# Layer 0's output weights split at later places, and layer 1's scores in fewer, wider products

## The chip, the cores and the metric

The kernel runs on one core of one Trainium2 chip. The metric is the device time of one execution in microseconds (us). The kernel before takes 779.3 us, the median of three runs (778.96 to 779.54).

## The reference, cut to what matters

The model is a two-layer backbone over 512 latent tokens and 256 context tokens with 1024 features. Layer 0 mixes latent attention (8 heads, softmax over all 768 tokens) with a bidirectional recurrence, gates both, and multiplies the 1024 mixed features by an output matrix. Layer 1 is a neighbourhood attention with 16 heads of 64: each latent token attends to a window of its grid (8 rows by 16 columns) and to all 256 context tokens, in one softmax:

```python
y_l = jnp.concatenate([o_l * jax.nn.silu(g_mla[:, c_:]), r_l * jax.nn.silu(g_lru[:, c_:])], axis=-1) @ w_out   # layer 0
...
s_loc = jnp.einsum('bhqd,bhrqcd->bhqrc', q_row, k_win) + bias                                                  # layer 1
s_ctx = jnp.einsum('bhqd,bhkd->bhqk', q_row, k_c)
s = jnp.concatenate([s_loc.reshape(b_, NA_HEADS, GRID_W, n_loc), s_ctx], axis=-1)
p = jax.nn.softmax(s.astype(jnp.float32), axis=-1)
```

## The kernel before, in words

All matrix products keep nearly float32 precision by splitting every operand into a high part (rounded by ScalarE, "ACT") and a low part (the remainder, subtracted by VectorE, "DVE", or by GpSimd, "POOL"). A product is then three products of TensorE ("PE"): high by high, high by low, low by high. Weights come from HBM as raw tiles by DMAs that SyncE's queue ("SP") issues, `load_w`, and are split by `split_raw`.

Raw weight tiles live in a pool with the tag "r", which has three buffers; high and low parts have the tags "h" and "l" with four buffers each. Layer 0's attention uses the same three tags in turn for its transposed probabilities (`pt_tile`, line 837: "rhl" by a running number). A tile takes a buffer when one is free.

Layer 0's attention runs head by head. `scores(hd, qt)` makes the products into PSUM (line 808), the row maximum on DVE (line 810), the exponential on ACT (line 812), and the normalization on POOL (line 764). `tail(hd, half, i)` takes one step of `mla_tail`: four transposes on PE (line 881), the split of the transposed tile on ACT (line 843) and DVE (line 844), and the products with the values (lines 861 and 862). The last step of a head combines the halves (lines 757 to 759) into the feature tile `mix`. `split0(p)` splits feature tile p into `mh` and `ml`; tile 3 comes from heads 6 and 7 and is the last. Between these calls stand the preparations of the output weights: the matrix is cut into four quarters `w0o[0]` to `w0o[3]` of 256 output features, each loaded and split in two pieces of four feature tiles (`w0o00`, `w0o04`) or in three pieces of three (`w0o20`, `w0o23`, `w0o26`). `out0(q, c)` then multiplies (line 1175), in the order of feature tiles 4, 5, 6, 7, 0, 1, 2, 3: the first four come from the recurrence and are ready early, so that these products can run between the last steps of the attention.

Layer 1's `scores1(hd, b)` handles 128 queries. `q2` holds their high and their low part in two slots, each doubled over both halves of the 128 rows; `k2` holds 512 latent and then 256 context keys, the high part in one half of the rows and the low part in the other. So each slot of `q2` meets both parts of the keys at once: 256 latent keys (line 1346) and the 256 context keys (line 1347), in two products into one PSUM tile of 512 columns. For b under 3 the latent keys are one stretch of 256; for b = 3 they are the first and the last 128.

The calls stand in a long hand-written order. A planner with its own model of time then orders the instructions of each engine: what stands earlier in the program goes first, but an instruction that the model holds to be not ready yet lets later ones pass. After that each engine works through its list strictly in order. `behind(ACT)` adds one rule: what is traced inside it on ACT comes after the ACT instruction traced last before it. `go(key)` runs a generator to its next `yield`, so a piece of work can be started in one place and continued in others.

Of the kernel before, what the change touches and what calls it, by code (L numbers as in the profile page):

```python
# [22 lines left out]
NL = 512  # L23
# [23 lines left out]
def build(nc, tc, A, out, dbg=None):  # L47
# [4 lines left out]
    V, S, P, G, SY = nc.vector, nc.scalar, nc.tensor, nc.gpsimd, nc.sync  # L52
    PE, ACT, DVE = mybir.EngineType.PE, mybir.EngineType.Activation, mybir.EngineType.DVE

    def f(ap):
        return ap.bitcast(F32)

    def dump(name, ap):
        if dbg is not None and name in dbg:
            SY.dma_start(dbg[name], ap)  # L60
# [14 lines left out]
    def tile3(p, tag, dt=F32, bufs=None):  # L75
        return lambda name, dt=dt: p.tile([128, NT], dt, tag=tag, name=name, bufs=bufs)
# [6 lines left out]
    th = tile3(ph, "th")  # L83

    def t4(name, shape=(1024,), dt=F32, tag="r", p=None):
        t = (p or pc).tile([128, 1024], dt, tag=tag, name=name, bufs=(PA if p else PC)[tag])
        n = int(np.prod(shape))
        if len(shape) == 1:
            return t[:, :n]
        names = "abc"[: len(shape)]  # L90
        return t[:, :n].rearrange(
            f"p ({' '.join(names)}) -> p {' '.join(names)}", **dict(zip(names, shape))
        )
# [3 lines left out]
    def small(tag, name, n=1, dt=F32):  # L97
        return sm.tile([128, n], dt, tag=tag, name=name, bufs=SM.get(tag))
# [14 lines left out]
    def load_w(name, src, shape, new=None):  # L113
        raw = (new or t4)(name + "r", shape, F32, "r")
        SY.dma_start(raw, src)
        return raw

    def split_raw(name, raw, shape, new=None, eng=V, heng=S):
        hi = (new or t4)(name + "h", shape, F32R, "h")
        if heng is S:  # L120
            S.activation(hi, raw, AF.Copy)
        else:
            heng.tensor_copy(hi, raw)
        lo = (new or t4)(name + "l", shape, F32R, "l")
        eng.tensor_tensor(lo, raw, f(hi), ALU.subtract)
        return hi, lo

    def split_w(name, src, shape, new=None, eng=V, heng=S):
        return split_raw(name, load_w(name, src, shape, new), shape, new, eng, heng)
# [68 lines left out]
    def behind(*engines):  # L198

        stack = ExitStack()  # L200
        for e in engines:
            stack.enter_context(tc.issue_after(next(i for i in reversed(nc.cur_bb.bb.instructions) if i.engine == e)))
        return stack
# [64 lines left out]
    def of3(tile):  # L268
        def new(n, s, dt, tag):
            if tag == "r":  # L270
                return t4(n, s, dt, tag)
            return tile(n, dt)[:, : s[0] * s[1]].rearrange("p (a b) -> p a b", b=s[1])

        return new
# [135 lines left out]
    def go(key, new=None):  # L410

        if new is not None:
            going[key] = new
        next(going[key], None)
# [85 lines left out]
    nl, e, z, w, q = (small("sp", f"sp{i}", 8) for i in range(5))  # L500
# [260 lines left out]
    def softmax_tail(p, rsum, name):  # L761
        rc = small("rc", name, 1)
        V.reciprocal(rc, rsum)  # L763
        G.tensor_scalar(p, p, rc, 0.5, ALU.mult, ALU.mult)  # L764
# [35 lines left out]
    def scores(hd, qt):  # L800
        qh, ql = qs[hd]
        kh, kl = KH[hd % 2], KL[hd % 2]
        if qt < 4:
            s = zz(f"s{hd}{qt}")
            qc = slice(128 * qt, 128 * qt + 128)
            for i, (a, b) in enumerate(((qh, kh), (qh, kl), (ql, kh))):
                for c in (LAT, CTX):
                    P.matmul(s[:, c], a[:96, qc], b[:96, c], start=(i == 0), stop=(i == 2))  # L808
            nm, rsum = small("nm", f"nm{hd}{qt}"), small("rs", f"rs{hd}{qt}")
            V.tensor_reduce(nm, s[:, :NT], AX.X, ALU.max, negate=True)  # L810
            p = th(f"p{hd}{qt}")
            S.activation(p, s[:, :NT], AF.Exp, bias=nm, accum_out=rsum)  # L812
            softmax_tail(p, rsum, f"rc{hd}{qt}")
            pts[hd, qt] = p
            return
        s = zz(f"sc{hd}")[:, :512]
        for qt in range(2):
            qc = slice(NL + 128 * qt, NL + 128 * qt + 128)
            for i, (a, b) in enumerate(((qh, kh), (qh, kl), (ql, kh))):
                P.matmul(  # L820
                    s[:, 256 * qt : 256 * qt + 256], a[:96, qc], b[:96, CTX],
                    start=(i == 0), stop=(i == 2),
                )
        nm, rsum = small("nm", f"nmc{hd}", 2), small("rs", f"rsc{hd}", 2)
        V.tensor_reduce(nm, s.rearrange("p (a b) -> p a b", a=2), AX.X, ALU.max, negate=True)
        p = ptmp.tile([128, 512], F32, tag="pcx", name=f"pc{hd}", bufs=1)
        for qt in range(2):
            S.activation(
                p[:, 256 * qt : 256 * qt + 256], s[:, 256 * qt : 256 * qt + 256], AF.Exp,
                bias=nm[:, qt : qt + 1], accum_out=rsum[:, qt : qt + 1],  # L830
            )
            softmax_tail(p[:, 256 * qt : 256 * qt + 256], rsum[:, qt : qt + 1], f"rcc{hd}{qt}")
        pts[hd, 4] = p
# [134 lines left out]
    v_t(5)  # L968
    scores(0, 2)
    mh, ml = [None] * 8, [None] * 8  # L970
    def wo_prep(l, name, q, new=None, step=4, eng=V, heng=S):
        w = []
        for k in range(0, 8, step):
            n = min(step, 8 - k)
            h, lo = split_w(f"{name}{q}{k}", A["wo"][l, q, :, k : k + n], (n, 256), new, eng, heng)
            w += [(h[:, i], lo[:, i]) for i in range(n)]
        return w

    def split0(p):
        mh[p], ml[p] = tl(f"mh{p}", F32R), (tl if p == 4 else tmix)(f"ml{p}", F32R)  # L980
        S.activation(mh[p], mix[p], AF.Copy)
        (V if p == 3 else G).tensor_tensor(ml[p], mix[p], f(mh[p]), ALU.subtract)
# [3 lines left out]
    def tail(hd, half, i):  # L986
        if i == 0:
            tails[hd, half] = mla_tail(hd, half)
        next(tails[hd, half], None)
# [7 lines left out]
    w0o = {}  # L997
# [6 lines left out]
    def w0o_prep(q, new=None, step=4):  # L1004
        w0o[q] = wo_prep(0, "w0o", q, new, step, G if q == 0 else V)
# [98 lines left out]
    tail(5, 1, 0)  # L1104
    tail(5, 1, 1)
    scores(6, 4)
    w0o_prep(0)
    split0(1)
    tail(5, 1, 2)
    go("a3")  # L1110
# [8 lines left out]
    scores(7, 2)  # L1119
    split0(7)  # L1120
    tail(6, 0, 2)
    tail(6, 0, 3)
    tail(6, 1, 0)
    tail(6, 1, 1)
    tail(6, 1, 2)
    tail(6, 1, 3)
    split0(2)
    scores(7, 3)
    scores(7, 4)
    w0o_prep(2, of3(th), 3)  # L1130
    tail(7, 0, 0)
    tail(7, 0, 1)
    tail(7, 0, 2)
    tail(7, 0, 3)
    tail(7, 1, 0)
    tail(7, 1, 1)
    tail(7, 1, 2)
    tail(7, 1, 3)
    split0(3)
    for p in range(8):  # L1140
        dump(f"mix{p}", mix[p])

# [11 lines left out]
    def st(name):  # L1154
        return ps_.tile([128, 512], F32, tag="s", name=name)
# [71 lines left out]
        w = (LAT, CTX)[c]  # L1227
        h_block(1, j, c, x1[j][:, w], rsb1[:, w], hh1[j], hl1[j], PIECES[c])

    w0o_prep(1)  # L1230
    out0(0, 0)
    w0o_prep(3, of3(tl), 3)
    out0(2, 0)
# [16 lines left out]
    def t2(tag, name, dt=F32, bufs=None):  # L1250
        return pn2.tile([128, 512], dt, tag=tag, name=name, bufs=bufs)
# [79 lines left out]

    p1 = {}

    def scores1(hd, b):
        q2, k2 = qk[hd], ke1[hd // 2][hd % 2]
        bt = bias[hd % 2]
        if b == 0:
            SY.dma_start(bt[:, :2], A["bias"][hd])
        s = st(f"s1{hd}{b}")
        for i in range(2):  # L1340
            lhs = q2[:, i, 128 * b : 128 * b + 128]
            if b < 3:
                kap = k2[:, 128 * b : 128 * b + 256]
            else:
                kap = k2[:, :NL].rearrange("p (a b) -> p a b", b=128)[:, ::3]
            P.matmul(s[:, :256], lhs, kap, start=(i == 0), stop=False, skip_group_check=True)  # L1346
            P.matmul(s[:, 256:], lhs, k2[:, CTX], start=False, stop=(i == 1), skip_group_check=True)  # L1347
        nm, rsum = small("nm", f"nm1{hd}{b}"), small("rs", f"rs1{hd}{b}")
        bb = bt[:, 0::2] if b < 3 else bt[:, 1:3]
        sv = s.rearrange("p (a b) -> p a b", b=256)  # L1350

        V.tensor_tensor_reduce(sv, sv, bb, -1.0, 3e38, ALU.add, ALU.min, nm)  # L1352
        p = t2("p", f"p1{hd}{b}", bufs=6)
        S.activation(p, s, AF.Exp, bias=nm, scale=-1.0, accum_out=rsum)  # L1354
        softmax_tail(p, rsum, f"rc1{hd}{b}")
        p1[hd, b] = p
# [45 lines left out]
    def w1o_prep(q, new=None, step=4, **kw):  # L1402
        w1o[q] = wo_prep(1, "w1o", q, new, step, **kw)
# [47 lines left out]
    v_t1(0, 4)  # L1451
    k1(0)
    scores1(0, 0)
    scores1(0, 1)
    scores1(0, 3)
    scores1(0, 2)
# [268 lines left out]
    for half, j0 in steps:  # L1725
# [6 lines left out]
        ks = [0, 3, 5, 2, 4, 1, 6, 7]  # L1732
# [109 lines left out]
```

## Time and profile before

| | before |
|---|---|
| median of three runs | 779.3 us (778.96 to 779.54) |
| the profiled execution | 780.51 us, its span 778.7 us |
| PE busy | 742.4 us (95% of the span) |
| DVE, ACT, POOL busy | 507.5, 415.6 and 163.7 us |
| granted PE clock | full in all but the last stretch |

The span runs from the first to the last instruction of the program; the execution's own time holds some 1.8 us around it. Busy time of PE counts overlapping products once. Starts are counted from the span's start. A line in an engine's timeline gives the start, the duration, what was done, how many in a row (x2), and in brackets how long the engine stood idle before it and whom it waited for.

### The profile page before, as it was taken

How to read it: one execution, taken by the hardware profiler on the slowest of the kernel's cores; microseconds unless marked ns; L12 is line 12 of the kernel's file. 1: busy time of each engine (PE TensorE's matmuls, PEld its weight loads, DVE VectorE, ACT ScalarE, POOL GpSimd, SP SyncE). 2: the span in 40 equal slices, each digit the busy share in tenths (PEclk: the TensorE clock that was granted, in tenths of full speed). 3: DMA queues.
4: the chain of work that ended last, by engine and by line, in shares of the span. 5: the costliest groups of instructions: out<-in, count | busy, mean ns of one | idle time of the engine just before them, and what ended most of it. 6: DMA issues, size and time to landing. Idle time of an engine off the chain costs nothing.

```text
span 778.7 us, 13220 instructions
## 1 busy us (share of the span) xinstructions
PE 742.4 (95%) x4966; PEld 652.8 (84%) x4966; DVE 507.5 (65%) x1051; ACT 415.6 (53%) x811; POOL 163.7 (21%) x191
## 2 busy tenths in 40 slices
PE   2999999999999999999999999999999999999995
PEld 2678898787788877888998899888888799889995
DVE  5748499887478777753396567546653766568544
ACT  5424867964467777542245355535542645456633
POOL 0000002003153477404210022002200211021414
PEclk9999999999999999999999999999999999999998
DMA  8913403411455553257021550236124541336203
GB/s 332 407 49 109 134 28 122 162 42 28 118 157 141 177 169 126 89 172 261 28 82 46 144 163 16 91 113 190 38 99 140 174 120 55 109 102 170 82 1 109
DMA packets 33598, 95.29 MB, mean 122 GB/s; under 512 B 4608, under 2 KB 6784, under 8 KB 33536
## 3 DMA queue, kind: packets, MB, share of 16 engines
q1 hardware_dynamic: 32960, 93.93, 37.5%
q8 instruction: 39, 0.64, 0.3%
q10 hardware_dynamic: 576, 0.52, 0.2%
q14 instruction: 23, 0.19, 0.1%
HBM read 73.99 MB, written 4.19 MB: 100 GB/s over the span
## 4 chain that ended last, share of the span: by engine, by line
PE 75%; DVE 12%; ACT 5%; issue 4%; DMA 3%; POOL 1%; SPq 0%; POOLq 0%; ACTq 0%; DVEq 0%
PE psg L141 11%; PE psv L1270 8%; PE psq L141 7%; PE w0oy L1175 7%; PE pskl L141 6%; PE psx L141 4%; PE w1oy L1175 4%; PE pt L1387 3%; PE pskc L141 3%; PE psada L215 2%; PE s L1346 2%; PE s L808 2%; PE s L1347 2%; PE po L1370 2%; PE po L1371 2%
## 5 line engine op out<-in xcount | busy, mean ns | idle before, releaser
L764 POOL TENSOR_SCALAR p<-p,rc 128x512 f32<-128x512 f32 (+1 forms) x96 | 77.7, 812 | 325.8 <-DVE rc L763 309.7
L1354 ACT ACTIVATE p<-s,nm 128x512 f32<-128x512 f32 x64 | 43.8, 686 | 37.0 <-DVE nm L1352 20.6
L1390 DVE TENSOR_TENSOR ptl<-pt,pth 128x512 fp32r<-128x512 f32 x64 | 43.6, 687 | 26.7 <-ACT pth L1389 26.7
L1389 ACT ACTIVATE pth<-pt 128x512 fp32r<-128x512 f32 x64 | 37.3, 595 | 34.7 <-PE pt L1387 25.5
L1352 DVE CUSTOM_DVE_ANT_1 s<-s,bias 128x512 f32<-128x512 f32 x48 | 33.2, 696 | 16.3 <-PE s L1347 14.3
L1387 PE MATMUL pt<-ident,p 128*128 128x128 f32 x256 | 40.0, 272 | 0.0
L615 POOL TENSOR_TENSOR mix<-mix,la 128x256 f32<-128x256 f32 x4 | 3.6, 905 | 172.8 <-DVE la L609 124.8
L844 DVE TENSOR_TENSOR pt<-pt,pt 128x512 fp32r<-128x512 f32 x48 | 31.9, 681 | 11.5 <-ACT pt L843 11.4
L843 ACT ACTIVATE pt<-pt 128x512 fp32r<-128x512 f32 x48 | 27.4, 595 | 16.1 <-PE pt L881 16.0
L763 DVE RECIPROCAL rc<-rs 128x1 f32<-128x1 f32 x96 | 15.2, 158 | 31.6 <-ACT p L1354 22.2
L1346 PE MATMUL s<-k,q 128*128 128x256 f32 x128 | 34.3, 292 | 0.4 <-DMA q<-qx 0.2
L812 ACT ACTIVATE p<-s,nm 128x768 f32<-128x768 f32 x32 | 28.8, 901 | 10.7 <-DVE nm L810 10.4
L1387 PEld LDWEIGHTS pt<-ident,p 128*128 128x128 f32 x256 | 31.1, 140 | 4.0 <-issue 0.4
L810 DVE TENSOR_REDUCE nm<-s 128x1 f32<-128x768 f32 x32 | 30.4, 951 | 4.6 <-PE s L808 4.1
L1347 PE MATMUL s<-k,q 128*128 128x256 f32 x128 | 33.3, 284 | 0.0
L1370 PE MATMUL po<-pth,v 128*128 128x256 f32 (+1 forms) x96 | 31.6, 335 | 0.0
L1371 PE MATMUL po<-ptl,v 128*128 128x256 f32 (+1 forms) x96 | 29.6, 324 | 0.0
L881 PE MATMUL pt<-ident,p 128*128 128x128 f32 x192 | 28.7, 273 | 0.0
L862 PE MATMUL po<-pt,v 128*128 128x256 f32 x96 | 26.1, 296 | 1.7 <-DVE pt L844 1.6
L861 PE MATMUL po<-pt,v 128*128 128x256 f32 x96 | 26.6, 294 | 0.4 <-DVE rcc L763 0.4
L1346 PEld LDWEIGHTS s<-k,q 128*128 128x128 f32 x128 | 24.3, 190 | 3.0 <-issue 1.4
L1200 ACT ACTIVATE sq<-xr 128x512 f32<-128x512 f32 (+1 forms) x16 | 8.2, 522 | 33.1 <-DVE xr L1181 27.1
(966 smaller groups left out, 2636.8 us busy)
## 6 DMA issues: line engine op xcount, KB each, us to landing
ada_0r<-ada SPq DMA_DIRECT2D x22, 512.0 KB, 5.0
ada_4r<-ada SPq DMA_DIRECT2D x22, 512.0 KB, 5.4
q<-qx SPq DMA_DIRECT2D x32, 256.0 KB, 5.0
bias<-bias SPq DMA_DIRECT2D x16, 256.0 KB, 2.7
x<-xin SPq DMA_DIRECT2D x8, 384.0 KB, 6.3
xr<-xin SPq DMA_DIRECT2D x8, 384.0 KB, 7.0
x1d<-xr SPq DMA_DIRECT2D x8, 256.0 KB, 5.2
x<-x1d SPq DMA_DIRECT2D x8, 256.0 KB, 4.2
```

The lines of the kernel that those rows point to most:

```text
L141: P.matmul(ps, a(k), b[k][:, c], start=(k == 0 and i == 0), stop=(k == nk - 1 and i == 2),)
L764: G.tensor_scalar(p, p, rc, 0.5, ALU.mult, ALU.mult)
L1175: P.matmul(ps, a, b[k][:, c], start=(n == m == 0 and ps is dst[0][0] and not second), stop=(n == 7 and m == 2), skip_group_check=True,)
L1270: P.matmul(ps, tok(a[k], t), b[:, k % 4], start=(k == 0 and i == 0), stop=(k == 7 and i == 2))
L1346: P.matmul(s[:, :256], lhs, kap, start=(i == 0), stop=False, skip_group_check=True)
L1347: P.matmul(s[:, 256:], lhs, k2[:, CTX], start=False, stop=(i == 1), skip_group_check=True)
L1354: S.activation(p, s, AF.Exp, bias=nm, scale=-1.0, accum_out=rsum)
L1370: P.matmul(dst, vv, h, start=first, stop=False, skip_group_check=True)
L1371: P.matmul(dst, vv, l, start=False, stop=last, skip_group_check=True)
L1387: P.transpose(ps[:, 128 * j : 128 * j + 128], p1[hd, b][:, 128 * c : 128 * c + 128], ident)
L1389: S.activation(h, ps, AF.Copy)
L1390: V.tensor_tensor(l, ps, f(h), ALU.subtract)
```

## The change

The quarters 0, 2 and 1 of layer 0's output weights are prepared by a new generator. It issues the loads of all pieces at its first step. Each later step splits one piece, and the high part's ACT instruction is put behind the ACT instruction traced last at that place, unless its pin is 0. Quarter 0's first piece is split behind the ACT work of `tail(6, 0, 2)` and its second behind that of `tail(6, 1, 2)` (both before: free to run as soon as the planner holds them ready). Quarter 2's pieces come behind `tail(7, 0, 2)`, `tail(7, 1, 0)` and `tail(7, 1, 3)`. Quarter 1 is loaded after these, in place of just before `out0(0, 0)`; its first piece is free and its second is split behind `split0(3)`. Quarter 3 stays as it was. In layer 1, for b under 3, one product of 512 columns takes the place of two of 256: the moving operand is a view of `k2` with two stretches of 256 keys. The tile b = 3 keeps its two products.

```diff
+    def wo_prep2(l, name, q, new=None, step=4, eng=V, pins=(1, 1, 1)):
+        ks = range(0, 8, step)
+        ns = [min(step, 8 - k) for k in ks]
+        raws = [load_w(f"{name}{q}{k}", A["wo"][l, q, :, k : k + n], (n, 256), new) for k, n in zip(ks, ns)]
+        yield
+        w0o[q] = []
+        for k, n, raw, pin in zip(ks, ns, raws, pins):
+            with behind(ACT) if pin else ExitStack():
+                h, lo = split_raw(f"{name}{q}{k}", raw, (n, 256), new, eng)
+            w0o[q] += [(h[:, i], lo[:, i]) for i in range(n)]
+            yield
...
     scores(6, 4)
-    w0o_prep(0)
+    go("w0o", wo_prep2(0, "w0o", 0, eng=G))
     split0(1)
...
     tail(6, 0, 2)
+    go("w0o")
     tail(6, 0, 3)
...
     tail(6, 1, 2)
+    go("w0o")
     tail(6, 1, 3)
     split0(2)
     scores(7, 3)
     scores(7, 4)
-    w0o_prep(2, of3(th), 3)
+    go("w0o2", wo_prep2(0, "w0o", 2, of3(th), 3))
     tail(7, 0, 0)
     tail(7, 0, 1)
     tail(7, 0, 2)
+    go("w0o2")
     tail(7, 0, 3)
     tail(7, 1, 0)
+    go("w0o2")
     tail(7, 1, 1)
     tail(7, 1, 2)
     tail(7, 1, 3)
+    go("w0o2")
+    go("w0o1", wo_prep2(0, "w0o", 1, pins=(0, 1)))
+    go("w0o1")
     split0(3)
+    go("w0o1")
...
-    w0o_prep(1)
     out0(0, 0)
     w0o_prep(3, of3(tl), 3)
...
+    def halves3(ap, a):
+        return ap.rearrange("p (a b) -> p a b", a=a)
...
             if b < 3:
-                kap = k2[:, 128 * b : 128 * b + 256]
-            else:
-                kap = k2[:, :NL].rearrange("p (a b) -> p a b", b=128)[:, ::3]
+                kap = (
+                    halves3(k2, 3)[:, ::2], halves3(k2, 2)[:, :, 128:384], halves3(k2, 3)[:, 1:]
+                )[b]
+                P.matmul(s.rearrange("p (a b) -> p a b", b=256), lhs, kap, start=(i == 0), stop=(i == 1))
+                continue
+            kap = k2[:, :NL].rearrange("p (a b) -> p a b", b=128)[:, ::3]
             P.matmul(s[:, :256], lhs, kap, start=(i == 0), stop=False, skip_group_check=True)
             P.matmul(s[:, 256:], lhs, k2[:, CTX], start=False, stop=(i == 1), skip_group_check=True)
```

## Rows read from the trace of the kernel before

**Rows 1.** Busy time by stretch: us, each engine's busy us (x instructions), PE clock, DMA.

```profile
300.00:320.00 20.00, 17.75 (x144) 15.27 (x145) 14.86 (x32) 16.71 (x36) 15.39 (x15) 1.00 0.29 91
...
440.00:720.00 280.00, 279.25 (x1850) 248.86 (x1849) 172.77 (x378) 142.30 (x301) 44.20 (x59) 1.00 0.36 110
```

**Rows 2.** PE's waits over the whole span: total us, times, longest us.

```profile
PE s L808 <- ACT p L812: 3.0, 3, 1.8
...
PE w0oy L1175 <- ACT mh L981: 0.6, 1, 0.6
```

**Rows 3.** Timeline of PE around 305 us.

```profile
304.46 0.60 PE L881 MATMUL pt<-ident,p 128*128 128x128 f32 x4
306.90 0.62 PE L808 MATMUL s<-kh,qh 96*128 96x512 f32 x2 [1.85 <-ACT p L812]
...
319.49 0.47 PE L1175 MATMUL w0oy<-mh,w0o04h 128*128 128x512 f32 x1
```

**Rows 4.** Timeline of ACT in the same stretch.

```profile
302.18 1.06 ACT L121 ACTIVATE w0o00h<-w0o00r 128x1024 fp32r<-128x1024 f32 x1 [0.23 <-DMA w0o00r<-wo]
...
304.91 1.06 ACT L121 ACTIVATE w0o04h<-w0o04r 128x1024 fp32r<-128x1024 f32 x1 [1.41 <-DMA w0o04r<-wo]
305.88 0.88 ACT L812 ACTIVATE p<-s,nm 128x768 f32<-128x768 f32 x1
...
310.77 1.07 ACT L843 ACTIVATE pt<-pt 128x512 fp32r<-128x512 f32 x2
...
317.11 0.60 ACT L843 ACTIVATE pt61c<-pt61c 128x512 fp32r<-128x512 f32 x1 [0.46 <-PE pt61c L881]
```

**Rows 5.** Timeline of DVE in the same stretch.

```profile
303.12 2.02 DVE L810 TENSOR_REDUCE nm<-s 128x1 f32<-128x768 f32 x2 [0.45 <-PE s L808]
...
319.38 1.02 DVE L125 TENSOR_TENSOR w0o20l<-w0o20r,w0o20h 128x768 fp32r<-128x768 f32 x1 [0.57 <-ACT w0o20h L121]
```

**Rows 6.** Timeline of POOL in the same stretch.

```profile
306.05 2.39 POOL L125 TENSOR_TENSOR w0o04l<-w0o04r,w0o04h 128x1024 fp32r<-128x1024 f32 x1 [0.35 <-ACT w0o04h L121]
308.40 0.92 POOL L764 TENSOR_SCALAR p<-p,rc 128x768 f32<-128x768 f32 x1
...
318.67 0.93 POOL L764 TENSOR_SCALAR pc<-pc,rcc 128x256 f32<-128x256 f32 x2 [0.63 <-PE po L862]
```

**Rows 7.** Chain that ended last, in order of time: start us, us, what.

```profile
300.60 4.23 DMA w0o04r<-wo
...
339.21 1.07 ACT w0o14h L121
340.30 1.22 DVE w0o14l L125
...
343.57 0.85 ACT mh L981
```

**Rows 8.** Timeline of ACT, late in the attention.

```profile
326.13 0.60 ACT L843 ACTIVATE pt<-pt 128x512 fp32r<-128x512 f32 x1 [3.53 <-PE pt L881]
```

**Rows 9.** Timeline of SP's queue in the same stretch.

```profile
324.70 0.33 SPq L115 DMA_DIRECT2D w0o10r<-wo  x1
...
341.93 4.67 SPq L1162 DMA_DIRECT2D xr<-xin  x8
```

**Rows 10.** Timeline of PE: first product with the second quarter.

```profile
354.16 0.39 PE L1175 MATMUL w0oy<-mh,w0o14h 128*128 128x512 f32 x1
```

**Rows 11.** Timeline of PE in layer 1: 20 products of 512 columns, then 8 score products.

```profile
597.81 0.40 PE L141 MATMUL pskl<-h1h,w1k5h 128*128 128x512 f32 x1
...
598.28 0.39 PE L141 MATMUL pskl<-h1h,w1k5l 128*128 128x512 f32 x1
...
602.37 0.28 PE L141 MATMUL pskc<-h1h,w1k5h 128*128 128x256 f32 x1
...
602.85 0.28 PE L1346 MATMUL s<-k,q 128*128 128x256 f32 x1
...
603.80 0.38 PE L1387 MATMUL pt<-ident,p 128*128 128x128 f32 x2
```

## The prediction, made before the changed kernel ran

> **What bounds the kernel now.** I read busy time by stretch first. In layer 1 TensorE (PE) is busy for 279.25 of 280 us; around 300 us, in the last third of layer 0's attention, for only 17.75 of 20, while ScalarE (ACT) there is busy for 16.71 and POOL for 15.39 [rows 1]. So layer 1 is bound by how long the products take on PE, and what an edit saves there comes off the end. In layer 0 the question is which waits PE has. Its list of waits gives the longest in this region: 1.8 of the 3.0 us in which the scores of line 808 wait for an exponential on ACT. One of 0.6 stands further on, where the last output products wait for the split of the last feature tile [rows 2]. Both lie where the change works.
>
> The timelines tell what made the first. PE begins its last transposes at 304.46 and then stands idle for 1.85 us until 306.90 [rows 3]. ACT in that time splits `w0o00` (1.06 us from 302.18), then stands for 1.41 us because the raw `w0o04` has not landed, splits it (1.06 from 304.91), and only then makes the exponential, at 305.88 [rows 4]. Its maximum came from DVE: two reductions of 2.02 us together from 303.12, so the first was ready at about 304.1 [rows 5]. The load that ACT waited for was under way for 4.23 us from 300.60 [rows 7]. ACT works strictly in order, so a weight that nobody needs until 319.49 [rows 3] held up a score that PE needed at once.
>
> For the second wait I follow the chain of waits: ACT splits `w0o14` for 1.07 us from 339.21, DVE subtracts for 1.22 from 340.30, and only after that DVE combines the last head, and the split of its feature tile comes at 343.57 [rows 7]. That weight is first used at 354.16 [rows 10].
>
> **The change part by part.** The sum is made against the profiled execution, 780.51 us with a span of 778.7; the median of the runs is 779.3, so 1.2 us go off at the end.
>
> *First stall.* The two splits of quarter 0 leave the place at 302 to 306. Without them the exponential could start at about 304.1, when its maximum is there, and its 0.88 us end at 305.0; PE has transposes until 304.46 + 0.60 = 305.06. So the 1.85 us go almost whole; what is late next is the maximum, by about 0.1. I take -1.75 (bounds: 0, if the planner puts other work on ACT there, to -1.85).
>
> *Where these splits go.* The first comes behind the copy of `tail(6, 0, 2)`, the second of the two copies from 310.77, and the second behind `pt61c` at 317.11 [rows 4]. Between them ACT has almost no idle time, so 1.06 us are inserted where PE needs its results; but ACT arrives there some 1.8 us earlier. Behind the waiting split stand the exponentials and copies of heads 6 and 7, and behind those PE. On POOL the subtraction takes 2.39 us, and already before it held a normalization back until 308.40; POOL then works for head 6 and 7 until 318.67 + 0.93, with few gaps [rows 6]. Heads 6 and 7 were scored well ahead of their transposes, which covers this mostly. I take +0.4 (0 to 1.06 for each of the two splits, 2.1, if that cover is gone).
>
> *Late filler.* Before, PE could begin output products at 319.49 [rows 3]; these fill its time until the next transposes. Now the second split ends at about 317.1 - 1.8 + 0.6 + 1.06 = 317.0 and its low part 2.39 later, at 319.4, in a time that is 1.8 shorter: PE wants it at 317.7. It has steps of head 7 to do meanwhile. I take +0.2 (0 to 1.8).
>
> *Quarter 2.* Its splits no longer stand between the first steps of head 7, but each behind one. On ACT they hit idle time: at 326.13 ACT had waited 3.53 us for PE [rows 8]. But the first step issues three loads at once, and these take all three buffers of tag "r". The second copy of head 7 needs one too. It has to wait until `w0o20` is split (behind the third copy) and subtracted: about 0.85 us on ACT (by its size between the 0.60 of a copy and the 1.06 of `w0o04`) and 1.02 on DVE [rows 4, 5]. Output products of quarter 0 cover that, if they are ready. I take +0.2 (0 to 3.2, see the slower rival).
>
> *Quarter 1 and the end of the attention.* Its second split is now behind `split0(3)`, so 1.07 + 1.22 us leave the chain ahead of the last combination [rows 7]. PE feels at most its 0.6 us wait there [rows 2]. In exchange the last piece of quarter 2 is split behind the combination's ACT work; its subtraction, below the 1.02 of `w0o20`, can fall between DVE's additions, and products with it are not there to fill time. I take -0.4 (-0.6 to +1.0). The two loads of this quarter (one stood at 324.70 before) go to SP's queue ahead of the eight loads of `xr`, which took 4.67 us to issue from 341.93 [rows 9]; they have to find free "r" buffers, and what is queued behind them, quarter 3 and `xr`, waits for them. Against their first use at 354.16 [rows 10] the 13 us cover that; I take nothing (0 to +1).
>
> *Scores of layer 1.* 48 tiles (16 heads by three) change from four products of 256 columns to two of 512. Eight score products took 603.80 - 602.85 = 0.95 us, or 0.475 for four. Twenty products of 512 columns took 602.37 - 597.81 = 4.56 us, or 0.456 for two [rows 11]. The saving is 0.019 us a tile and 0.9 in all. The first two of the twenty took 0.47, that is 0.005 a tile and 0.2 in all; without them the other 18 took 4.09, or 0.454 for two and 1.0 in all. A loss is not excluded either: a first product of 512 after a wait may start its successor later than one of 256 does, but of the rows read none shows two of 256 as cheaper, so I end the bounds at +0.1. I take -0.9. DVE's additions get their scores no later.
>
> The Trainium skill, "TensorE: Matmul & The Clock Gate", section "Back-to-back issue gap", gives a fixed 2.5 ns on top of the columns for each product at full clock; joining two would save only that, 96 times, 0.24 us in all as an estimate. The rows differ: two of 256 take 0.2375 and one of 512 takes 0.228, so about 9.5 ns. Since this case's rows have both shapes side by side, the sum goes by them.
>
> The sum: -1.75 + 0.4 + 0.2 + 0.2 - 0.4 - 0.9 = -2.25 us, so 780.51 becomes 778.3, and the median 779.3 - 2.25, about **777.0**.
>
> **The rivals.**
>
> *The wait in layer 0 only moves.* ACT (16.71 of 20) and POOL (15.39 of 20) [rows 1] are nearly full in this stretch; take away PE's 1.85 us of idle time and the same work stands in 18 us. Then the exponentials or normalizations are late somewhere else, and layer 0 gives nothing. Against it: 1.41 us of what ACT lost was a wait for a load, not work [rows 4]. Only the scores remain: 779.3 - 0.9 = 778.4.
>
> *The wide scores bring nothing.* If a product is bound by its columns alone, two of 256 and one of 512 cost the same, and layer 0 alone remains: -1.35, which is 777.95. For it speaks the 0.47 of the first two in rows 11, against it the 18 that follow. The rule of "TensorE: Matmul & The Clock Gate" above would have this come out near it.
>
> *Slower: head 7 starves for "r" buffers.* The second and the fifth copy of head 7 need an "r" buffer while quarter 2's raw pieces hold all three, and these are let go only behind the copies of other steps. Each such turn costs split, subtraction and the copy's own two halves: 0.85 + 1.02 + 0.60 + 0.7 = 3.2 us, in a chain on which the last feature tile and so the end of layer 0 hang. It decides once output products of quarter 0 don't cover it, that is when the low part of `w0o04` comes more than about 3 us after 317.7. Both turns uncovered: 6.4 - 2.25 = +4.1, 783.4; one uncovered, 3.2 - 2.25 = +1.0, 780.3. For it: POOL's load. Against it: ACT had 3.53 us of idle time there [rows 8], and quarter 0 offers 42 products of 512 columns for its first two feature tiles, 42 times 0.228, or 9.6 us of cover.
>
> **How the numbers follow.** A measurement of this kernel can tell a difference of about 0.2%, 1.56 us, so faster means under 777.74. The forecast has 0.57, with its own range of 775.3 to 778.3 (all gains whole and no new wait make -1.85 - 0.6 - 1.0 = -3.45, or 775.85, and half a microsecond is added below because the planner orders later work anew); 0.53 of it is faster, 0.04 within. The moved wait has 0.16, all within. The scores without gain have 0.10, half faster and half within. The slower rival has 0.17, of which 0.15 is slower, over 780.86, and 0.02 (one turn) within. That makes faster 0.58, within 0.27, slower 0.15. The range goes up to the slower rival's one uncovered turn and leaves out the two, and down to a little below the best sum: 774.9 to 780.3.
>
> **What would show it.** Right: no PE wait near 305 us, ACT with no wait for a raw `w0o04`, the score products at 0.455 us for two, and layer 1's PE busy time about 1 us shorter for the same work. The 0.6 us wait for the last feature tile is shorter. Wrong: a new PE wait for line 843 or 844 in head 7, DVE's `w0o20` subtraction or POOL's `w0o04` subtraction just before it, SP waiting long for a buffer with `xr` behind it, or products of 512 columns at 0.24 us.

## The result, and the profile after

The changed kernel takes 772.48 us (median of four runs, 771.64 to 772.77), against 779.13 for the kernel before. The ratio is 0.9914, with a 95% interval of 0.9897 to 0.9931: 6.65 us faster (5.4 to 8.0). Forecast were 777.0 with a range of 774.9 to 780.3, so the direction was right and the size much too small. The profiled execution took 771.64 us with a span of 769.8.

The busy time in the stretches of [rows 1], after the change:

```profile
300.00:320.00 20.00, 19.25 (x131) 17.18 (x132) 16.89 (x32) 15.77 (x33) 15.58 (x14) 1.00 0.26 79
...
440.00:720.00 280.00, 279.80 (x1790) 246.87 (x1789) 175.81 (x385) 145.51 (x306) 47.43 (x63) 1.00 0.38 113
```

PE is now busy for 19.25 of the 20 us around 300, where it had 17.75. The list of PE's waits from 290 to 440 us (total, times, longest) says why; the 1.8 and the 0.6 us of [rows 2] are gone:

```profile
PE psv L1290 <- DVE h1l L341: 0.7, 1, 0.7
PE psq L141 <- ACT w1q0h L121: 0.5, 1, 0.5
PE pt L881 <- DVE cbc L758: 0.4, 1, 0.4
PE po L862 <- DVE pt L844: 0.3, 1, 0.3
```

The timeline of PE, answering [rows 3]: twelve transposes run straight into the scores, with no wait, and the first output product is there 3.5 us earlier. Of these, 1.9 lie ahead of this stretch, as shown below.

```profile
304.79 1.48 PE L881 MATMUL pt<-ident,p 128*128 128x128 f32 x12
306.02 0.59 PE L808 MATMUL s<-kh,qh 96*128 96x512 f32 x2
...
316.00 0.47 PE L1196 MATMUL w0oy<-mh,w0o04h 128*128 128x512 f32 x1
```

The timeline of ACT, answering [rows 4, 7]. The splits of quarter 0 stand behind copies that PE has already been given, and neither waits for its load. At the end of the attention the order is turned round: `mh`, the last feature tile, comes ahead of the split of `w0o14`.

```profile
304.84 0.90 ACT L812 ACTIVATE p<-s,nm 128x768 f32<-128x768 f32 x1
...
306.69 1.06 ACT L121 ACTIVATE w0o00h<-w0o00r 128x1024 fp32r<-128x1024 f32 x1
...
312.68 1.05 ACT L121 ACTIVATE w0o04h<-w0o04r 128x1024 fp32r<-128x1024 f32 x1
...
336.03 0.85 ACT L994 ACTIVATE mh<-mix 128x768 fp32r<-128x768 f32 x1 [1.89 <-DVE mix L759]
336.79 1.04 ACT L121 ACTIVATE w0o14h<-w0o14r 128x1024 fp32r<-128x1024 f32 x1
```

To see where the time went I cut both spans at the same products: from the transposes of `pt51c` to the first key product of layer 1 (the first line of each fence), and from there to the last transposes (the second). The columns are those of [rows 1]. The kernel before:

```profile
298.20:427.00 128.80, 124.38 (x813) 110.87 (x812) 73.69 (x150) 57.50 (x113) 36.32 (x33) 1.00 0.32 111
427.00:742.30 315.30, 314.55 (x2099) 281.82 (x2099) 190.88 (x411) 159.15 (x333) 53.41 (x68) 1.00 0.37 113
```

The changed kernel:

```profile
296.30:421.90 125.60, 123.47 (x813) 110.47 (x812) 74.90 (x150) 57.10 (x113) 36.15 (x33) 1.00 0.34 114
421.90:733.60 311.70, 311.50 (x2002) 275.96 (x2002) 189.88 (x411) 159.91 (x333) 53.35 (x68) 1.00 0.38 114
```

The tail of layer 0 is 3.2 us shorter for the same 813 products: PE's idle time fell from 4.42 to 2.13, and its busy time from 124.38 to 123.47. Layer 1 is 3.6 us shorter, 3.05 of it busy time. The end gives 0.2. The two profiled spans differ by another 1.9 us, ahead of these stretches, in code that both kernels share. That part changes from one execution to the next (the last section shows how) and is left out of the account: 3.2 + 3.6 + 0.2 = 7.0, which lies inside the measured interval.

### The profile page after: what moved, and what is told of

Its sections match the earlier page's. It is cut to its first block, busy times and chain, and to the rows that moved or that the text cites. A ratio compares the mean times of both kernels' runs of the same rounds, so it can differ in the third digit from the quotient of the medians.

```text
span 769.8 us, 13043 instructions
## 1 busy us (share of the span) xinstructions
PE 736.6 (96%) x4870; PEld 646.2 (84%) x4870; DVE 508.0 (66%) x1051; ACT 416.2 (54%) x811; POOL 163.4 (21%) x191
## 4 chain that ended last, share of the span: by engine, by line
PE 78%; DVE 11%; ACT 5%; issue 4%; DMA 1%; POOL 1%; SPq 0%; POOLq 0%; ACTq 0%; DVEq 0%
PE psg L141 11%; PE psv L1290 9%; PE w0oy L1196 8%; PE psq L141 7%; PE pskl L141 6%; PE psx L141 5%; PE w1oy L1196 4%; PE pt L1414 3%; PE s L1370 3%; PE pskc L141 3%; PE s L808 2%; PE psada L215 2%; PE po L1397 2%; PE po L1398 2%; PE pt L881 2%
## 5 line engine op out<-in xcount | busy, mean ns | idle before, releaser
L1416 ACT ACTIVATE pth<-pt 128x512 fp32r<-128x512 f32 x64 | 37.5, 595 | 30.9 <-PE pt L1414 23.1
L1370 PE MATMUL s<-k,q 128*128 128x512 f32 x96 | 31.2, 409 | 0.2
L758 DVE TENSOR_TENSOR cb<-po,cb 64x512 f32<-64x512 f32 (+1 forms) x25 | 16.6, 666 | 17.4 <-ACT cb L757 17.0
L757 ACT ACTIVATE cb<-po 64x512 f32<-64x512 f32 (+1 forms) x25 | 14.3, 572 | 18.8 <-PE po L1398 17.6
```

Of the source, the lines that this page charges most:

```text
L1370: P.matmul(s.rearrange("p (a b) -> p a b", b=256), lhs, kap, start=(i == 0), stop=(i == 1))
L1416: S.activation(h, ps, AF.Copy)
```

## The experiments

Two theories stood at first. By one, the parts add up: the scores' width gives its 0.9, and the rest is layer 0's waits. The rival: layer 1 gains because the planner, whose model holds the wide scores to be cheaper, puts layer 1's other work in another order. All kernels below ran beside the kernel before on the same chip, and each has its own ratio. Gains in microseconds are the ratio times the median of the kernel before. "Stretch" is the first line of the fences above, measured in each run's one profile.

**The scores alone**, layer 0 as before.

```diff
-                kap = k2[:, 128 * b : 128 * b + 256]
...
+                kap = (
+                    halves3(k2, 3)[:, ::2], halves3(k2, 2)[:, :, 128:384], halves3(k2, 3)[:, 1:]
+                )[b]
+                P.matmul(s.rearrange("p (a b) -> p a b", b=256), lhs, kap, start=(i == 0), stop=(i == 1))
+                continue
```

> The kernel before with the wide score products alone; layer 0's output weights are split where they were. Between the first product of layer 1's keys (line 141, pskl) and the last score product the changed kernel's profile gained 3.6 us over the one before, where 0.9 was forecast. Whatever its cause, if it belongs to the score edit alone, this kernel has all of it: about 779.1 - 3.6 = 775.5 us, with layer 0 as before (first pskl at about 427 us, less what the start of a run varies). If it needs layer 0's change too, it is near the forecast's 778.2.

Measured: 0.9946 (0.9934 to 0.9959), that is 4.2 us, more than four times the forecast for the scores. Layer 1 from its first key product to the last transposes takes 311.48 us where the kernel before has 315.34.

**The wide scores in the old order.** The planner's order of the kernel before was written out as a table of runs for all five engines, and each instruction was tied behind the one ahead of it in the table, with no semaphore. In the traces PE, ACT, DVE and POOL then work in the order of the kernel before, the scores apart. The table follows the instructions' numbers in the program; two old score products share one place.

```diff
+ORDER = {
+    "PE": [
+        (10, 8), (0, 4), (8, 2), (18, 8), (4, 4), (27, 2), (26, 1), (29, 16), (100, 2), (45, 13),
...
+        for e, runs in order.items():
+            seq = [own[e][k] for a, n in runs for k in range(a, a + n)]
+            for p, i in zip(seq, seq[1:]):
+                tc.add_manual_dep(
...
+    pin(ORDER)
```

> The same wide products, but every engine's instructions are tied to the order that the planner had made for the kernel before (each wide product stands where the first of its two narrow ones stood). Theory 'width': one product of 512 for two of 256 is itself worth all 3.6 us, by fewer starts after waits; then 775.5 us. Theory 'order': width alone is worth the forecast's 0.9 us, and the rest comes from the new order that the planner makes when the scores cost it less; then 778.2 us, and PE's losses at starts after waits and around the conditioning products (line 215) are those of before.

**The narrow scores in the new order.** The counterpart: the products of before, tied in the order that the planner made for the wide ones (again the traces show it kept).

```diff
+ORDER = {
...
+        (2626, 1), (2492, 8), (2581, 1), (2583, 1), (2585, 1), (2587, 1), (2589, 1), (2591, 1), (2593, 1), (2595, 1),
...
+    pin(ORDER)
```

> The counterpart: the kernel before with its narrow products, every engine tied to the order that the planner makes for the wide ones. Theory 'width': no gain, 779.1 us. Theory 'order': all but the width's 0.9 us, that is 3.6 - 0.9 = 2.7 us less than before, 776.4 us.

Measured: the width in the old order gives 0.9993 (0.9979 to 1.0008), 0.5 us with an interval that holds zero; the new order without the width gives 0.9967 (0.9956 to 0.9978), 2.6 us. So the larger part of the scores' gain is not their width. The two don't sum to the 4.2 of both, but their intervals are wide enough for it. Layer 1, from its first key product to the last transposes, takes 313.86 us with the width alone and 312.84 with the order alone; the eight profiles with the old order and narrow scores have 314.9 to 317.1. The groups of score products, busy time and mean ns, in the kernel before and in the changed one:

```profile
L1346 PE MATMUL s<-k,q 128*128 128x256 f32 x128 | 34.3, 292 | 0.4 <-DMA q<-qx 0.2
L1347 PE MATMUL s<-k,q 128*128 128x256 f32 x128 | 33.3, 284 | 0.0
```

```profile
L1370 PE MATMUL s<-k,q 128*128 128x512 f32 x96 | 31.2, 409 | 0.2
L1373 PE MATMUL s<-k,q 128*128 128x256 f32 x32 | 8.6, 287 | 0.0
L1374 PE MATMUL s<-k,q 128*128 128x256 f32 x32 | 8.5, 285 | 0.0
```

Busy times of single products overlap, so I counted the time from a product's start to the next product's start. Without the three or four score products that a conditioning product follows, the scores' sum is 31.71 us before, 30.71 after, 30.60 with the wide scores in the old order, and 31.62 with the narrow ones in the new: the width is worth 1.1 us in the old order and 0.9 in the new. With those few products in, it is 32.35, 31.90, 31.46 and 32.45, and the width is worth 0.9 and 0.6. What the order changes shows most in the conditioning products of layer 1's gate (`psada`), 64 products in two groups. Kernel before, and then changed kernel:

```profile
L215 PE MATMUL psada<-ada_0r,c 128*32 128x256 f32 x32 | 5.8, 387 | 0.0
L215 PE MATMUL psada<-ada_4r,c 128*32 128x256 f32 x32 | 4.4, 387 | 0.0
```

```profile
L215 PE MATMUL psada<-ada_4r,c 128*32 128x256 f32 x32 | 4.1, 385 | 0.0
L215 PE MATMUL psada<-ada_0r,c 128*32 128x256 f32 x32 | 3.8, 388 | 0.0
```

The busy times sum to 10.2 us before and 7.9 after, but overlaps are in them. Counted from the first start of a run of these products to the start of the product behind it, the 64 take 6.17 us before, in eight runs of 2 to 22, and 5.09 after, in six. In the timeline of PE in the kernel before they lie between scores, transposes and others, and after a change of kind the next product starts late: 608.55 to 608.67 is the 0.12 of one score, but from the last score at 608.67 to the conditioning product it is 0.21. In all eight runs it is 0.20 to 0.33.

```profile
608.55 0.28 PE L1346 MATMUL s<-k,q 128*128 128x256 f32 x1
608.67 0.28 PE L1347 MATMUL s<-k,q 128*128 128x256 f32 x1
608.88 0.63 PE L215 MATMUL psada<-ada_0r,c 128*32 128x256 f32 x4
609.44 0.39 PE L1346 MATMUL s<-k,q 128*128 128x256 f32 x1
609.66 0.28 PE L1347 MATMUL s<-k,q 128*128 128x256 f32 x1
```

**Test of that: the conditioning products together.** The order of before, tied, with one difference: the 32 products of each of the two groups stand together, at the place of the last of them.

```diff
+ORDER = {
...
+        (2626, 1), (2492, 1), (2496, 1), (2493, 3), (2497, 3), (2581, 1), (2583, 1), (2585, 1), (2587, 1), (2589, 1),
...
+    pin(ORDER)
```

> The kernel before, every engine tied to its own old order, but the 32 products of each of layer 1's two conditioning groups (line 215, psada of the gate) stand together, at the place of the last of them, in place of being mixed with other products. The time around these products was 8.0 us in layer 1 before and 6.7 in the changed kernel; a group that stands together took 1.86 us in layer 0. Theory 'order': the mixing itself costs, so 1.5 to 3 us less than before and no new PE waits. If the products only fill time that PE would stand idle, no gain, and waits appear in their old places.

Measured: 0.9959 (0.9947 to 0.9972), 3.2 us, with the narrow scores and the old layer 0. The groups in this kernel:

```profile
L462 PE MATMUL psada<-ada_0r,c 128*32 128x256 f32 x32 | 2.5, 385 | 0.0
L462 PE MATMUL psada<-ada_4r,c 128*32 128x256 f32 x32 | 2.5, 379 | 0.0
```

Counted from start to start, the 64 take 3.73 us in two runs of 32, where it was 6.17; the traces show every other instruction of PE, ACT, DVE and POOL in the order of before. So mixing them with other products costs time, and the planner's new order, with 5.09, had taken back only part of it. No run ties the kernel before to its own order with nothing else changed, so what the ties do by themselves stays open.

**The three edits of layer 0 alone**, the scores as before: the first half of the change.

```diff
-    w0o_prep(0)
+    go("w0o", wo_prep2(0, "w0o", 0, eng=G))
...
-    w0o_prep(2, of3(th), 3)
+    go("w0o2", wo_prep2(0, "w0o", 2, of3(th), 3))
...
+    go("w0o1", wo_prep2(0, "w0o", 1, pins=(0, 1)))
```

> The edits of layer 0's output weights alone, with the narrow scores. The changed kernel's profile gained 3.2 us between the fifth head and the end of layer 0, where 1.35 was forecast. If layer 0's edits alone make this, 779.1 - 3.2 = 775.9 us; if the forecast's price was right and the rest is the variation between two profiles, 777.8 us.

Measured: 0.9949 (0.9934 to 0.9964), 4.0 us (4.2 between the medians). Its stretch is 125.6 us, as in the changed kernel; the five runs with the old layer 0 (the kernel before, the scores alone, and the three tied kernels with the old layer 0) have 128.8 to 129.7, mean 129.3. So layer 0 gives 3.7 and not 1.35. The next kernels ask which edit brings it.

**Quarter 0 alone, quarter 1 alone, quarter 2 alone.**

```diff
-    w0o_prep(0)
+    go("w0o", wo_prep2(0, "w0o", 0, eng=G))
```

> The kernel before with quarter 0's edit alone (both pieces split behind tail(6,0,2) and tail(6,1,2)). The three edits of layer 0 together took 4.2 us off (780.3 to 776.1). Theory 'stall': the wait of PE near 305 us and the jam on ACT and POOL behind it carry this, so quarter 0 alone gives 2.5 to 3 us, about 777.5. Theory 'three parts': the gain is spread, quarter 0 gives only the wait itself, 1.5 to 1.9 us, 778.5.

```diff
+    go("w0o1", wo_prep2(0, "w0o", 1, pins=(0, 1)))
+    go("w0o1")
     split0(3)
+    go("w0o1")
...
-    w0o_prep(1)
```

> Quarter 1's edit alone (loaded before the end of the attention, second piece split behind the last feature tile). Theory 'stall': at most the 0.6 us wait for the last feature tile, 779.6. Theory 'three parts': taking 2.3 us of split out of the chain to the last feature tile is worth over 1 us, 779.0 or less.

```diff
-    w0o_prep(2, of3(th), 3)
+    go("w0o2", wo_prep2(0, "w0o", 2, of3(th), 3))
```

> Quarter 2's edit alone (three loads at once, three splits spread over head 7). Theory 'stall': nothing, 780.3. Theory 'three parts': head 7's copies no longer stand behind the splits, about 1 us, 779.2. The slower rival of the forecast (head 7 waits for buffers of tag r): 780.3 + 1 or more.

Measured: quarter 0 gives nothing, 1.0000 (0.9991 to 1.0008), where both theories had a gain; quarter 1 is 1.2 us faster, 0.9984 (0.9975 to 0.9993); quarter 2 is 3.6 us slower, 1.0046 (1.0033 to 1.0059). Alone they sum to +2.4, together they make -4.0.

In quarter 0's kernel the stall near 305 us is gone, but another comes. The timelines, all engines mixed in order of time:

```profile
315.21 2.34 POOL L125 TENSOR_TENSOR w0o04l<-w0o04r,w0o04h 128x1024 fp32r<-128x1024 f32 x1
...
316.05 2.32 DVE L125 TENSOR_TENSOR w0o20l<-w0o20r,w0o20h 128x768 fp32r<-128x768 f32 x1 [0.50 <-ACT w0o20h L121]
...
318.29 0.41 DVE L758 TENSOR_TENSOR cbc<-poc,cbc 64x256 f32<-64x256 f32 x1
...
318.76 0.99 PE L881 MATMUL pt<-ident,p 128*128 128x128 f32 x4 [2.94 <-DVE cbc L758]
```

PE waits for the combination `cbc`, which stands on DVE behind the subtraction of `w0o20`; quarter 2's edit, not made here, would have put that behind the urgent work. And the subtraction takes 2.32 us where [rows 5] have 1.02, while POOL subtracts `w0o04` at the same time (the last section takes this up). The wait costs more than itself. The busy time and granted clock (the number before the last two) of PE after it, and later:

```profile
319.00:322.00 3.00, 3.00 (x10) 2.52 (x9) 3.00 (x6) 2.05 (x4) 3.00 (x4) 0.50 0.24 87
323.00:326.00 3.00, 3.00 (x15) 2.47 (x14) 0.69 (x2) 0.00 (x0) 0.00 (x0) 1.00 0.35 111
```

From 319 to 322 us the granted clock is 0.50, that is 1.2 GHz in place of 2.4, and 10 products are run where the same time later holds 15. Summed over half-microsecond windows (busy time times the missing share of the clock), 1.7 us are lost. This count is used below too, and is rather an upper bound, as the section on the prediction shows.

In quarter 2's kernel, ACT's queue ends in a load that comes late. The slower rival had copies of head 7 wait for an "r" buffer; here it is the load of quarter 1 that does:

```profile
337.01 1.06 ACT L121 ACTIVATE w0o10h<-w0o10r 128x1024 fp32r<-128x1024 f32 x1 [1.92 <-DMA w0o10r<-wo]
338.09 0.38 ACT L757 ACTIVATE cbc<-poc 64x256 f32<-64x256 f32 x1
...
338.98 0.63 ACT L121 ACTIVATE w0o26h<-w0o26r 128x512 fp32r<-128x512 f32 x1
```

SP issued that load only at 333.10, when an "r" buffer came free; it landed 3.89 us later. PE waits for the last split in this list:

```profile
339.66 0.65 PE L1191 MATMUL w0oy<-mh,w0o26h 128*128 128x512 f32 x1 [3.16 <-ACT w0o26h L121]
```

Behind that wait the clock is at half again, for 1.7 us of loss. 3.16 + 1.7 = 4.9 us at most for one such wait; the rival had 3.2 for one of its turns.

**Two at a time: quarters 0 and 2, quarters 0 and 1.**

```diff
-    go("w0o1", wo_prep2(0, "w0o", 1, pins=(0, 1)))
-    go("w0o1")
...
+    w0o_prep(1)
```

> Quarters 0 and 2 together, quarter 1 as before. Alone, quarter 0 gained 2.9 us up to the end of head 6 and lost 2.9 in a new wait of PE (its transposes waited for a combination on DVE behind the subtraction of w0o20, which took 2.3 us while POOL subtracted w0o04); quarter 2 alone lost 3.6, of which PE stood 3.2 for w0o26, tied behind a copy that stood behind the late load of w0o10. Theory 'each cures the other': quarter 2 takes w0o20 out of the way, the 2.9 stay gained; the wait for w0o26 needs quarter 1's edit to go, since it moves w0o10: then 780.6 - 2.9 + 3.6 = 781.3. If the wait for w0o26 goes without it, 777.7.

```diff
-    go("w0o2", wo_prep2(0, "w0o", 2, of3(th), 3))
+    w0o_prep(2, of3(th), 3)
```

> Quarters 0 and 1 together, quarter 2 as before. The subtraction of w0o20 still stands ahead of the combination while POOL subtracts w0o04, so quarter 0 gives nothing and quarter 1 its 1.2: 779.4. If quarter 1 is what frees quarter 0's gain, 776.5.

Measured (both diffs are against the kernel with all three): 1.0034 (1.0022 to 1.0047) and 1.0012 (0.9999 to 1.0024). Without quarter 2's edit the 2.94 us wait of quarter 0 alone is back, to the digit; in this profile PE also waits 1.57 us at 676.6 in layer 1 for the load of a query tile, as in no other, so its time is not layer 0's alone. Quarters 1 and 2 were not run as a pair. Without quarter 1's, ACT and PE at the end of the attention:

```profile
334.00 1.06 ACT L121 ACTIVATE w0o14h<-w0o14r 128x1024 fp32r<-128x1024 f32 x1 [3.34 <-DMA w0o14r<-wo]
335.08 0.38 ACT L757 ACTIVATE cbc<-poc 64x256 f32<-64x256 f32 x1
...
335.97 0.63 ACT L121 ACTIVATE w0o26h<-w0o26r 128x512 fp32r<-128x512 f32 x1
```

```profile
336.65 0.80 PE L1193 MATMUL w0oy<-mh,w0o26h 128*128 128x512 f32 x1 [3.77 <-ACT w0o26h L121]
```

The untied split of `w0o14` stands ahead of the last combination and waits 3.34 us for its load. In the full change it is tied behind `mh` and can hold nothing up.

**The same without the tie.** All three edits, with every pin at 0.

```diff
-    go("w0o", wo_prep2(0, "w0o", 0, eng=G))
+    go("w0o", wo_prep2(0, "w0o", 0, eng=G, pins=(0, 0)))
...
+    go("w0o2", wo_prep2(0, "w0o", 2, of3(th), 3, pins=(0, 0, 0)))
...
+    go("w0o1", wo_prep2(0, "w0o", 1, pins=(0, 0)))
```

> All three edits of layer 0 with the same places and loads, but no split is tied behind ACT's work (all pins 0). If the tie makes the gain, the planner moves the splits forward again as before, and the time goes back towards 780.3. If the later place in the program does, it stays near 776.1; the planner's order then differs on ACT in the place of the splits of quarter 0 and little else.

Measured: 1.0022 (1.0013 to 1.0031), 1.7 us slower than before, so the later place without the tie makes no gain. The planner puts the split of `w0o00` at 304.53, ahead of `cbc` and `cb`, and PE waits twice:

```profile
308.56 0.97 PE L881 MATMUL pt<-ident,p 128*128 128x128 f32 x4 [2.03 <-DVE cbc L758]
...
322.54 1.12 PE L881 MATMUL pt<-ident,p 128*128 128x128 f32 x4 [1.92 <-DVE pt L844]
```

Both waits are followed by half the clock (1.7 and 1.6 us lost). The early splits bring POOL's subtractions forward, and DVE stands beside them. Ahead of the first wait:

```profile
305.67 2.36 POOL L125 TENSOR_TENSOR w0o00l<-w0o00r,w0o00h 128x1024 fp32r<-128x1024 f32 x1 [0.15 <-ACT w0o00h L121]
306.56 1.48 DVE L250 TENSOR_TENSOR am<-am,vec 128x4 f32<-128x4 f32 x1
```

An operation on 4 elements ends when POOL does, and `cbc` starts on DVE only behind it, at 308.08. Ahead of the second wait, the subtraction of `w0o20` takes 2.80 us beside POOL's `w0o04`.

**The changed order with the conditioning products together.** The changed kernel's order, tied, with the conditioning products of layer 1's gate in two runs of 32.

```diff
+ORDER = {
...
+        (2614, 1), (2492, 4), (2569, 1), (2571, 1), (2573, 1), (2575, 1), (2577, 1), (2579, 1), (2581, 1), (2583, 1),
...
+    pin(ORDER)
```

> The changed kernel, every engine tied to its own order, with the same two groups put together. Theory 'order': 1 to 2 us less than the changed kernel, so about 7.5 to 9 us under the kernel before on this chip. If mixing costs nothing, 6.7 to 8 us under it, as the changed kernel.

Measured: 0.9884 (0.9867 to 0.9901) of the kernel before, where the change has 0.9914 (0.9897 to 0.9931). They ran on different chips and the intervals overlap, so the two ratios alone don't part them. One profile of each points the same way: layer 0's stretch is the same 125.6 us in the same order, and layer 1 takes 309.5 where the changed kernel has 311.8, with 3.75 in place of 5.09 for the 64 products.

## Why the prediction was wrong

*First stall: right.* 1.75 were forecast, and the 1.85 us are gone whole. What is late next costs little: PE now waits 0.3 us for a subtraction of line 844, where it waited 0.2 before.

*Quarter 1 and the end: right in kind.* -0.4 was forecast, the whole 0.6 went, since `mh` is now ahead of the split. Alone this edit gives 1.2 (0.5 to 1.9).

*The prices of the inserted work: too high.* For the inserted splits, the late filler and quarter 2 together I had +0.8. The waits after show 0.4 for `cbc`, and 0.4 of small waits of before (for `pt61c` and `xr`) are gone: together 0. PE's idle time in the stretch fell by 2.3 (4.42 to 2.13) where the sum had 1.35. The low part of `w0o04` did not come late for PE either: the first product that uses it starts at 317.32.

*No term for busy time in layer 0, or for what follows a wait.* Two pieces were missing. In the stretch, 0.9 us of busy time went for the same products. Why is not shown; it is not that fewer products change shape, for they do so 102 times after and 95 before. And the stall at 305 us has a hidden price in some executions of the old layer 0: in the scores-only run and in the one with narrow scores in the new order, the clock was at half behind it, and in the profiled run of before it was not. All five work off this stretch in the same order; without PE's idle time the two take 125.4 and 125.6 us, the three others 124.4 to 124.5, so the half clock cost 0.9 to 1.3 where the count by windows has 1.7. This is part of what separates the profile's 3.2 from the 3.7 against the mean of five runs.

*The step that failed most: "0.9 in all" for layer 1.* The term for the width was about right (0.6 to 1.1 measured), but the sum took layer 1's order as given and allowed half a microsecond for "the planner orders later work anew". The new order was worth 2.5: layer 1's total is 315.34 before, 312.84 with the narrow scores in the new order, 311.76 after. Counted from start to start over all of layer 1, the conditioning products make 1.1 of these 2.5 (6.17 to 5.09), the products of the attention with the values (`po`) 0.9, of which 0.4 is a wait that is gone, and those that make the values (`psv`) 0.5; every other kind changes by 0.2 or less. The first was tested by itself, the others were not.

*The slower rival: its turn came, and was covered.* In the full change a copy of head 7 does wait 2.40 us for the subtraction of `w0o20`:

```profile
320.66 0.60 ACT L843 ACTIVATE pt<-pt 128x512 fp32r<-128x512 f32 x1 [2.40 <-DVE w0o20l L125]
```

The turn is as the prediction had it, though the subtraction takes 2.28 us and not its 1.02. PE has no wait there, as output products fill the time. The slower kernels, quarter 2 alone and quarters 0 and 2, lost by a neighbouring path that the prediction did not name: quarter 1's late load holds up the split of `w0o26` (waits of PE of 3.16 and 3.77). In the full change the loads come late as well (ACT waits 3.35 us for `w0o10` from 325.5), but behind it stands nothing that PE then waits for: `w0o14`, the next, is tied behind `mh`. The prediction priced each edit by itself and added; the measured singles (0.0, -1.2, +3.6) show that no such sum exists here. Each edit moves the wait into the place that another edit clears.

*The rivals "the wait only moves" and "the wide scores bring nothing"* are both out: the stretch fell by 3.2 to 3.7 us, and the width is worth 0.6 to 1.1, counted by starts, in either order.

## What to carry to other kernels

When a planner orders the program, an edit that makes one kind of instruction cheaper in its model reorders everything behind it; compare the orders of the untouched stages before giving the gain to the edit, by tying each version to the other's order. Where splits must not hold up urgent work, tie them behind it: here a later place alone was slower than before. Edits on the same in-order queue are tried together, not only one by one, because each may only move the wait that another removes.

## What the hardware showed that was not expected

**Half the clock can follow a short wait of PE.** In the kernel with the scores alone, PE waited 1.38 us at 304.7 and then had the clock at 0.51:

```profile
307.00:310.00 3.00, 3.00 (x15) 2.82 (x14) 2.88 (x7) 2.94 (x7) 2.92 (x3) 0.51 0.12 36
```

The kernel before waited longer, 1.85 us [rows 3], and from 307 to 309 us its clock was at 1.00. Waits of 1.28 and 1.75 us were followed by half the clock, others of 1.43, 1.81 and 2.07 were not; all six waits of 1.9 us and more outside this place were, at about 1.7 us each by the count (2.65 behind the 3.77 one), and one of 1.57 us in layer 1 was not. So the length of the wait alone does not decide it. The Trainium skill, "TensorE: Matmul & The Clock Gate", section "What's actually happening", says that full clock is not the default: the engine runs at half unless recent activity releases it, and there are only these two levels. The windows agree with the two levels (0.50 and 1.00).

**DVE and POOL hold each other up.** The subtraction of 768 elements on DVE takes 0.96 us alone (`w0o23` in the changed kernel) and 2.28 here:

```profile
318.29 2.28 DVE L125 TENSOR_TENSOR w0o20l<-w0o20r,w0o20h 128x768 fp32r<-128x768 f32 x1
318.47 1.28 POOL L759 TENSOR_TENSOR mix<-mix,cb 64x512 f32<-64x512 f32 x1
```

It ends 0.82 us after POOL's addition does. In all nine slow cases of these runs, 1.94 to 2.80 us long and beside POOL instructions of 1.26 to 2.38, the end lies 0.82 to 0.84 us after that of POOL's instruction, as if DVE had stood still until then. The other way round, POOL's addition takes 2.00 us in place of 1.28 at 322.12 in the kernel before, where DVE had begun a subtraction 0.26 us earlier. In the changed kernel the subtraction stands behind the urgent copies, so this costs PE nothing. The Trainium skill, "GPSIMD Engine Reference", section "Specifications", says that POOL shares its SBUF interfaces with VectorE and names VectorE's instructions with two SBUF inputs among those that contend; the subtraction is one, and the numbers agree.

**The start differs from one execution to the next.** Eight conditioning products near 24 us took 0.85 us in the profiled execution of before (24.39 to 25.24) and 0.46 in that of the changed kernel, by the same code:

```profile
24.39 1.08 PE L215 MATMUL psada<-ada_0r,c 128*32 128x256 f32 x8
25.24 1.08 PE L215 MATMUL psada<-ada_4r,c 128*32 128x256 f32 x8
```

```profile
23.97 0.64 PE L215 MATMUL psada<-ada_0r,c 128*32 128x256 f32 x8
24.43 0.61 PE L215 MATMUL psada<-ada_4r,c 128*32 128x256 f32 x8
```

The view of busy time prints a granted clock of 1.00 for both, but the trace's record of the clock begins only at 26.89 us in the kernel before, and at 23.76 in the changed one; ahead of it nothing is on record. In the kernel before, eight of these products take 0.85 us just ahead of the record's start and 0.57 behind it. The first gate product of layer 0 starts at 31.0 us there. In the one experiment whose record begins as late, at 27.02, it starts at 30.9; in all others the record begins between 21.1 and 24.5, and it starts at 29.4 to 29.9. By this pace PE came to its full clock later in these two executions, which makes 1.6 of the 1.9 us; the statement that the clock of the kernel before was full in all but the last stretch does not hold for its start. What sets the moment stays open.
